# The low halves of streamed weights, made by a negated copy and an adding DMA in place of a subtraction

## The chip, the cores and the metric

The kernel runs on one core of one Trainium2 chip. The time is device microseconds of one execution of the program; fewer is better. The engines of the core are TensorE (PE in the profile), VectorE (DVE), ScalarE (ACT), GpSimd (POOL) and SyncE (SP, which only issues DMAs here). Each has its own queue of instructions and works through it in order; an instruction that waits for a semaphore holds up all that stands behind it on its engine.

## The reference

One layer of a hybrid backbone over 1,024 latent tokens of width 1,024 and 256 context tokens, all in fp32. What matters here is where its matrix products lie:

```python
u = h * (1 + sc1) + sh1                            # modulated tokens
p = u @ w_in + b_in                                # 1024 x 9280: q, k, v, o, gates of mLSTM and GLA
h_m = bidirectional mLSTM (8 heads of 128) of silu(short_conv(q, k)), v, gates
h_g = bidirectional GLA   (4 heads, 128 keys, 256 values) of q, k, v, decay
y_m = (head_norm(h_m) * sigmoid(o)) @ w_branch_mlstm
y_g = (head_norm(h_g) * silu(z)) @ w_branch_gla
mix = (sigmoid(gate_a) * y_m + sigmoid(gate_b) * y_g) @ w_out
h = layer_norm(ALPHA * h + g1 * mix)
gate, val = split((h * (1 + sc2) + sh2) @ w_up + b_up)      # D_FF = 2816
f = (gelu(conv3x3(gate)) * val) @ w_down + b_down
out = layer_norm(ALPHA * h + g2 * f)
```

## The kernel before

Each large product is made of three: both factors are split into a high part (the fp32 value rounded to the type that TensorE multiplies fast, written fp32r) and a low part (what the rounding left), and TensorE adds up high by high, high by low and low by high in one PSUM bank. `mm3` does this over the blocks of 128 rows; its three matmuls are lines 288, 289 and 290 of the profile (1083 to 1085 in the down projection).

Weights are streamed from HBM by `wload`. A call fetches one column block of 256 of a weight matrix in parts of two row blocks. For each part it takes a `raw` tile (four of them in a ring), SyncE loads it (256 KB, line 268), ScalarE copies it into a tile of the ring of `whi` (six tiles, the high part, line 257), and VectorE subtracts: raw minus high, into a tile of the ring of `wlo` (six, the low part, line 258). Each is 128 x 512. Most calls have four parts, because the inner dimension is 1,024; those of the down projection have one. 314 parts go into the two rings; eight parts of `w_out` and the last six parts of `w_down` go into tiles of their own (`s`, `u`, `wlate`), and all 328 pass through `raw`. With six tiles in a ring and four parts in a call, parts 0 and 1 of the next call find a free tile early, and parts 2 and 3 wait until TensorE has read parts of the call before.

The stages follow one another: modulation and log gates (to 230 us), four GLA heads (230 to 545), eight mLSTM heads in pairs (545 to 1115: a value projection for a pair, then query and key for each head, `ml_scan` between), output gates and branches (1115 to 1530), output projection (to 1630), the 22 blocks of the gated unit with its 3x3 convolution on VectorE (1630 to 2110), and the down projection (from 2110), whose last two column blocks are done by token tiles.

The order of instructions on each engine is not the order of the code: the framework's scheduler places them by its own estimate of when each can start, and it also gives out the tiles of a ring in that order. So a change of one instruction's engine moves others.

`split` also serves other places (the gated heads, `kk`, `qq`, `s`; ScalarE and GpSimd, also lines 257 and 258), which are not touched. In the mLSTM, `ml_scan` has GpSimd multiply and add tiles of 128 x 1024 (lines 695, 699, 701), ScalarE take exponentials (698, 702), and VectorE run short chains of Newton steps on 128 x 8 (`mrs`, lines 238 to 243).

Of the kernel before, what the change touches and what calls it, by code (L numbers as in the profile page):

```python
# [6 lines left out]
F32 = mybir.dt.float32  # L7
# [22 lines left out]
EPS = 1e-5  # L30
# [6 lines left out]
def layer_kernel(ctx, tc, I, out, dbg=None):  # L37
# [26 lines left out]
    def slot(i, shape, dt=F32):  # L64
        # 8, 9 and 10, 11 are halves of one tile each, taken in this order
        if i in (8, 9, 10, 11) and sl is sl0:
            n = 1
            for w in shape[1:]:
                n *= w
            tag = "kk" if i < 10 else "qq"  # L70
            if i % 2 == 0:
                half[tag] = sl.tile([P, 2, n], dt, tag=tag, name=nm(tag))
            v = half[tag][0:shape[0], i % 2, :]
            return v if len(shape) == 2 else v.rearrange("p (a b) -> p a b", b=shape[2])
        return sl.tile(shape, dt, tag=f"s{i}", name=nm(f"s{i}"))
# [10 lines left out]

    # ---------------------------------------------------------------- constants
    scn = ExitStack()
# [20 lines left out]

    # masks  # L110
    V.tensor_tensor(xi[:], ti[:], si[:], op=ALU.bitwise_xor)
# [11 lines left out]

    # small vectors, gathered as rows and turned into columns on the tensor engine
    pk0 = [(I["c"][0], 8), (I["c_ctx"], 8), (I["b_mod"][0:2048], 16)]
# [22 lines left out]

    # ---------------------------------------------------------------- modulation for the token mixing
    list(pack(pk0, 0))  # L150
# [20 lines left out]

    # gates, one row of the projection for each: the 32 of the linear attention three times, the 32 of the mLSTM
    raw = slot(7, [P, KD, P])
# [41 lines left out]

    # biases and norm factors in the scaled form in which they are used
    V.tensor_scalar(colB[:, c_om:c_om + 8], colB[:, c_om:c_om + 8], 0.5, None, op0=ALU.mult)
# [8 lines left out]

    # convolution of the bias with the taps, and what the taps beyond the ends would add
    cvb = cst.tile([P, 3, 16], F32, name="cvb")
# [6 lines left out]

    # ---------------------------------------------------------------- helpers
    def newton(y, v, tmp):
# [9 lines left out]
    def rsqrt1(y, h, var, tmp):  # L247
        # of one column, with h = -(var + EPS) / 2
        V.tensor_scalar(h, var, EPS, -0.5, op0=ALU.add, op1=ALU.mult)
        V.tensor_scalar(y.bitcast(I32), h.bitcast(I32), -0.5, float(0x5F3759DF - (1 << 30) - (1 << 22)),  # L250
                        op0=ALU.mult, op1=ALU.add)
        for _ in range(3):
            V.scalar_tensor_tensor(tmp, y, h, y, op0=ALU.mult, op1=ALU.mult)
            V.scalar_tensor_tensor(y, tmp, 1.5, y, op0=ALU.add, op1=ALU.mult)
# [5 lines left out]
    def wload(segs, nk=KD, k0=0, eng=V, into=None):  # L260
        parts = []
        for k4 in range(0, nk, 2):
            n = min(2, nk - k4)
            raw = stg.tile([P, 2, 256], F32, tag="raw", name=nm("raw"), bufs=4)
            r0 = (k0 + k4) * P
            wid = 0
            for src, c0, w, dst in segs:
                SY.dma_start(raw[:, 0:n, dst:dst + w],
                             src[r0:r0 + n * P, c0:c0 + w].rearrange("(k p) c -> p k c", p=P))
                wid = max(wid, dst + w)  # L270
            if into is None:
                hi = stg.tile([P, 2, 256], F32R, tag="whi", name=nm("whi"), bufs=6)
                lo = stg.tile([P, 2, 256], F32R, tag="wlo", name=nm("wlo"), bufs=6)
            else:
                hi, lo = (t[k4 // 4][:, k4 % 4:k4 % 4 + 2, :] for t in into)
            split(hi[:, 0:n, 0:wid], lo[:, 0:n, 0:wid], raw[:, 0:n, 0:wid], eng)
            parts.append((hi, lo))

        def w(k, c, n):
            hi, lo = parts[k // 2]  # L280
            return hi[:, k % 2, c:c + n], lo[:, k % 2, c:c + n]
        return w
# [8 lines left out]

    # ---------------------------------------------------------------- modulated tokens, channel-major, split
    uh = [ubt(k, [P, SEQ], F32R) for k in range(KD)]
# [33 lines left out]

    # ---------------------------------------------------------------- gates
    L = SEQ + CTX
    gr = slot(6, [96, L], F32R)  # L330
    gm = slot(15, [P, L])
    for b in range(3):
        for k in range(KD):
            if b < 2:
                c_ = slice(b * 512, b * 512 + 512)
                make_u(xt[4 * b:4 * b + 4], k, uh[k][:, c_], ul[k][:, c_], 0)
            else:
                make_u(ct, k, cuh[k // 4][:, k % 4, :], cul[k // 4][:, k % 4, :], 1)
        p = proj(lambda k, c, n: tuple(t[:, k % 4, :] for t in gwt[k // 4]), 0, b)
        # high parts, low parts, high parts  # L340
        o = slice(b * 512, b * 512 + BW[b])
        A.activation(gr[0:96, o], p[0:96, 0:BW[b]], AF.Identity, bias=gb[0:96, :])
        V.scalar_tensor_tensor(gr[32:64, o], p[32:64, 0:BW[b]], gb[32:64, :], gr[32:64, o].bitcast(F32),
                               op0=ALU.add, op1=ALU.subtract)
        A.activation(gm[96:128, o], p[96:128, 0:BW[b]], AF.Identity, bias=gb[96:128, :])

    # weights of the log forget gates of the gated linear attention: high, high, low parts
    gws = []
# [12 lines left out]
    def log_gates(h):  # L361
        # by direction, then the context of both
        for parts in (((0, 0), (0, 1)), ((1, 0), (1, 1)), ((0, 2), (1, 2))):
# [22 lines left out]
    def ml_gates():  # L386
        # gates of the mLSTM: rows of the two directions, each in its own storage order
        lf = slot(8, [64, L])
# [66 lines left out]

    # ---------------------------------------------------------------- projections
    def vbias(off):
# [47 lines left out]
    def gla_scan(h, q, k, v):  # L505
# [3 lines left out]
        for d in range(2):  # L509
            SY.dma_start(et[d][:], la_d[d][h][:])  # L510
            A.activation(et[d][:], et[d][:], AF.Exp, scale=1.0 / TAU)
            V.tensor_tensor(qq[:, d, :], et[d][:, 0:SEQ], q[:], op=ALU.mult)
        # context: what is left of the decay after each position
        ze = zero[:].to_broadcast([P, CTX - 1])
# [7 lines left out]
        A.activation(kk[:, 1, 0:SEQ], k[:, 0:SEQ], AF.Copy)  # L522
        # scores inside a chunk: blocks of hs positions against their sibling, from small to large;
        # q carries the decay from its block's border, k the decay to it
        am = slot(12, [P, 8, P])
# [7 lines left out]
        def pairs(t, d0, hs, o, n):  # L533
            # of 2 * hs positions the first half from direction d0, the second from the other one
            a = t[:, d0, o:o + 1]
# [4 lines left out]
        for l in range(7):  # L540
# [13 lines left out]
            for d, eng in ((0, V), (1, G if l % 2 else V)):  # L554
# [7 lines left out]
                eng.tensor_tensor(e4[:, :, 0, 0], e4[:, :, 0, 0], e4[:, :, 1, 0], op=ALU.mult)  # L562
        # whole chunks
        dec2 = sc.tile([P, 2, 8], F32, tag="gdec", name=nm("gdec"), bufs=2)
# [3 lines left out]
        for c0 in (8, 0, 4):  # L568
            for t in (sf, sb):
# [4 lines left out]
                A.activation(t[:, c0 * P:(c0 + n) * P].rearrange("p (c t) -> p c t", t=P), p[:, 0:n, :], AF.Copy)  # L574
        # states
        sbs = [slot(13 + i, [P, 4, 256]) for i in range(2)]
# [20 lines left out]
        def heads(g):  # L597
# [11 lines left out]
            for i in range(4):  # L609
                sq = sc.tile([P, 256], F32, tag="hn", name=nm("sq"), bufs=3)  # L610
                A.activation(sq[:], po[i // 2][:, i % 2, :], AF.Square, accum_out=ss[:, 0, i:i + 1])
            # 1 / sqrt(mean + EPS), with one step of Newton after the tables
            h_, y, m = ss[:, 1, :], ss[:, 2, :], ss[:, 3, :]
# [37 lines left out]
    def ml_proj_qk(h):  # L651
        w = wload([(w_in, O_QM + h * P, P, 0), (w_in, O_KM + h * P, P, P)])
        res = []
        for i in range(2):
# [8 lines left out]
            for b in range(2 + i):  # L663
# [8 lines left out]
                if b == 1:  # L672
                    tap(o, ed[:], t0)
                    tap(o - 1, p[:, 0:1], t2)
                # no neighbour at the ends
                if b != 1:
# [137 lines left out]

    # ---------------------------------------------------------------- output gates, branches, merge
    md_d = drt("md_d", [4096])
# [55 lines left out]
    for j2 in range(4):  # L872
        w = wload([(I["w_branch_gla"], j2 * 256, 256, 0)])
        for e in range(2):
# [11 lines left out]
            mod_row(j, acc)  # L886
    # columns of the gated unit
    rowF = ubt(19, [P, 3, P])
# [40 lines left out]

    # ---------------------------------------------------------------- output projection, first norm  # L930
    lt = ExitStack()
# [82 lines left out]

    # ---------------------------------------------------------------- convolutional gated unit
    ft = ExitStack()
# [42 lines left out]

    # ---------------------------------------------------------------- down projection, second norm  # L1060
    fin = ctx.enter_context(tc.tile_pool(name="fin", bufs=1))
# [11 lines left out]

    # column blocks of one group of rows of w_down after the other, in chunks of two row tiles
    todo = [(g, cb_, k) for g, (k0, k1) in enumerate(((0, N_RES), (N_RES, NF))) for cb_ in range(4)
# [71 lines left out]

    # the last two column blocks, by token tiles
    ahead(len(todo) - len(late))
# [45 lines left out]
```

## Time and profile before

| | |
|---|---|
| median of 3 runs | 2389.48 us (2388.05 to 2392.11) |
| profiled execution, span | 2388.8 us |
| TensorE busy | 2272.9 us, 95% |
| VectorE busy | 1429.5 us, 60% |
| ScalarE busy | 693.9 us, 29% |
| GpSimd busy | 347.7 us, 15% |
| DMA | 231 MB moved, mean 97 GB/s |

The profile is one execution. Rows of its groups read: line, engine, operation, output from input, shape, count, then busy time, mean ns of one, then the engine's idle time just before these instructions and what ended most of it. Rows of the timeline begin with the start in us and the duration. A matmul's row can overlap the next one's, since they are pipelined.

### The profile page before, as it was taken

How to read it: one execution, taken by the hardware profiler on the slowest of the kernel's cores; microseconds unless marked ns; L12 is line 12 of the kernel's file. 1: busy time of each engine (PE TensorE's matmuls, PEld its weight loads, DVE VectorE, ACT ScalarE, POOL GpSimd, SP SyncE). 2: the span in 40 equal slices, each digit the busy share in tenths (PEclk: the TensorE clock that was granted, in tenths of full speed). 3: DMA queues.
4: the chain of work that ended last, by engine and by line, in shares of the span. 5: the costliest groups of instructions: out<-in, count | busy, mean ns of one | idle time of the engine just before them, and what ended most of it. 6: DMA issues, size and time to landing. Idle time of an engine off the chain costs nothing. (4 is left out here: it accounts for less than half of the span.)

```text
span 2388.8 us, 33413 instructions
## 1 busy us (share of the span) xinstructions
PE 2272.9 (95%) x13093; PEld 1970.4 (82%) x13093; DVE 1429.5 (60%) x2664; ACT 693.9 (29%) x1107; POOL 347.7 (15%) x240
## 2 busy tenths in 40 slices
PE   8899999999889888998999999999999999989998
PEld 3788897988788777886886788898888888879998
DVE  4867647274956838656345544576655565567557
ACT  2563233233212223122431233313333333320110
POOL 2101101021220302202110032101011000025300
PEclk9999999999999999999999999999999999999999
DMA  7341021212222212222356644512111222145511
GB/s 254 82 145 49 30 64 43 74 47 60 74 70 75 72 54 83 65 85 91 93 160 215 207 136 154 190 63 71 53 54 39 68 71 78 65 136 177 207 54 63
DMA packets 192351, 231.12 MB, mean 97 GB/s; under 512 B 18577, under 2 KB 149265, under 8 KB 192193
## 3 DMA queue, kind: packets, MB, share of 16 engines
q1 hardware_dynamic: 190321, 222.43, 29.5%
q0 software_dynamic: 1728, 6.29, 0.8%
q8 instruction: 103, 1.69, 0.3%
q14 instruction: 55, 0.45, 0.1%
q10 hardware_dynamic: 144, 0.26, 0.0%
HBM read 183.52 MB, written 45.25 MB: 96 GB/s over the span
## 5 line engine op out<-in xcount | busy, mean ns | idle before, releaser
L288 PE MATMUL pj<-u,whi 128*128 128x512 f32 (+1 forms) x848 | 327.7, 386 | 30.2 <-DVE s L677 21.4
L258 DVE TENSOR_TENSOR wlo<-raw,whi 128x512 fp32r<-128x512 f32 x314 | 230.0, 736 | 204.1 <-ACT whi L257 200.4
L257 ACT ACTIVATE whi<-raw 128x512 fp32r<-128x512 f32 x314 | 197.0, 631 | 481.4 <-PE pj L290 181.5
L289 PE MATMUL pj<-u,whi 128*128 128x512 f32 (+1 forms) x848 | 327.2, 386 | 4.4 <-POOL u L308 3.3
L290 PE MATMUL pj<-u,wlo 128*128 128x512 f32 (+1 forms) x848 | 325.4, 384 | 0.0
L288 PE MATMUL pj<-s,whi 128*128 128x512 f32 x784 | 305.6, 390 | 0.0
L290 PE MATMUL pj<-s,wlo 128*128 128x512 f32 x784 | 305.6, 390 | 0.0
L1047 DVE SCALAR_TENSOR_TENSOR acc<-g,colF,acc 128x945 f32<-128x945 f32 (+2 forms) x168 | 205.0, 1220 | 155.7 <-ACT acc L1038 153.5
L289 PE MATMUL pj<-s,whi 128*128 128x512 f32 x744 | 290.2, 390 | 2.3 <-POOL s L1002 2.3
L288 PE MATMUL pj<-whi,u 128*128 128x256 f32 x768 | 222.5, 290 | 18.1 <-DVE s L647 18.1
L289 PE MATMUL pj<-wlo,u 128*128 128x256 f32 x768 | 221.8, 289 | 2.8 <-DVE wlo L258 2.8
L290 PE MATMUL pj<-whi,u 128*128 128x256 f32 x768 | 221.7, 289 | 0.0
L288 PEld LDWEIGHTS pj<-u,whi 128*128 128x128 f32 x848 | 162.9, 192 | 60.2 <-issue 32.0
L289 PEld LDWEIGHTS pj<-u,whi 128*128 128x128 f32 x848 | 162.9, 192 | 35.5 <-POOL u L308 6.4
L290 PEld LDWEIGHTS pj<-u,wlo 128*128 128x128 f32 x848 | 162.6, 192 | 28.0 <-issue 0.9
L290 PEld LDWEIGHTS pj<-s,wlo 128*128 128x128 f32 x784 | 147.2, 188 | 32.4 <-issue 1.7
L288 PEld LDWEIGHTS pj<-s,whi 128*128 128x128 f32 x784 | 147.2, 188 | 31.9 <-issue 0.9
L289 PEld LDWEIGHTS pj<-s,whi 128*128 128x128 f32 x744 | 139.7, 188 | 33.6 <-POOL s L1002 3.6
L288 PEld LDWEIGHTS pj<-whi,u 128*128 128x128 f32 x768 | 150.6, 196 | 18.6 <-issue 18.6
L289 PEld LDWEIGHTS pj<-wlo,u 128*128 128x128 f32 x768 | 150.7, 196 | 3.0 <-DVE wlo L258 3.0
L290 PEld LDWEIGHTS pj<-whi,u 128*128 128x128 f32 x768 | 150.3, 196 | 0.0
L661 DVE SCALAR_TENSOR_TENSOR s<-pj,colB,s 128x511 f32<-128x511 f32 (+2 forms) x96 | 57.6, 611 | 62.3 <-ACT s L666 61.7
(463 smaller groups left out, 4513.5 us busy)
## 6 DMA issues: line engine op xcount, KB each, us to landing
u<-in_w_mod_dram SPq DMA_DIRECT2D x48, 512.0 KB
raw<-in_w_in_dram SPq DMA_DIRECT2D x96, 256.0 KB
raw<-in_w_up_dram SPq DMA_DIRECT2D x176, 128.0 KB
raw<-in_w_in_dram SPq DMA_DIRECT2D x96, 128.0 KB
raw<-in_w_down_dram SPq DMA_DIRECT2D x44, 256.0 KB
s<-rr SPq DMA_DIRECT2D x16, 512.0 KB
qq<-re SPq DMA_DIRECT2D x16, 512.0 KB
gl<-val SPq DMA_DIRECT2D x12, 512.0 KB
```

The source lines that it names most:

```text
L257: A.activation(hi, src, AF.Copy)
L258: eng.tensor_tensor(lo, src, hi.bitcast(F32), op=ALU.subtract)
L288: T.matmul(p, lh, rh, start=k == 0, stop=False)
L289: T.matmul(p, lh, rl, start=False, stop=False)
L290: T.matmul(p, ll, rh, start=False, stop=k == nk - 1)
L661: V.scalar_tensor_tensor(y[:, o:o + src.shape[1]], src, t, y[:, o:o + src.shape[1]], op0=ALU.mult, op1=ALU.add)
L1047: V.scalar_tensor_tensor(av, g[:, r0 + dy:r1 + dy, c0 + dx:c1 + dx], convw(3 * ky + kx, f), av, op0=ALU.mult, op1=ALU.add)
```

## The change

In `wload` the call of `split` goes. ScalarE makes the high part as before and then a second copy of it with the sign turned, into the low part's tile; then GpSimd issues a DMA from the raw tile to the low part's tile that adds what it carries to what lies there. The low part is now minus high plus raw. The argument that named the subtracting engine is no longer read there. (The comments that the diff also drops are left out.)

```diff
-            split(hi[:, 0:n, 0:wid], lo[:, 0:n, 0:wid], raw[:, 0:n, 0:wid], eng)
+            h_, l_, r_ = hi[:, 0:n, 0:wid], lo[:, 0:n, 0:wid], raw[:, 0:n, 0:wid]
+            A.activation(h_, r_, AF.Copy)
+            A.activation(l_, h_.bitcast(F32), AF.Copy, scale=-1.0)
+            G.dma_start(l_, r_, accum_op=ALU.add)
             parts.append((hi, lo))
```

Every line from there on moves down by three: L702 becomes L705, L865 becomes L868. The new instructions are L277 (high part), L278 (negation) and L279 (DMA). Counted over the program, VectorE loses 328 instructions of 128 x 512, ScalarE gains 328, GpSimd's queue gains 328 DMA issues; on TensorE 683 rows of its order stand elsewhere, on SyncE 108, most of them before 230 us, where the gates' instructions of heads and log decays are interleaved anew.

On ScalarE, before the first mLSTM head (about 543 us; `whi_725` and `whi_728` are parts 2 and 3 of a call, `s6_773` is the tile of which L702 takes the exponential once GpSimd has written it), before:

```order
L257 ACTIVATE whi_725_4710<-raw_724_4707 128x512
L702 ACTIVATE s6_773_5098<-s6_773_5098 128x1024
L257 ACTIVATE whi_728_4717<-raw_727_4714 128x512
L257 ACTIVATE whi_749_4909<-raw_748_4906 128x512
L257 ACTIVATE whi_752_4916<-raw_751_4913 128x512
L666 ACTIVATE s0_730_4721<-pj_731_4722,cvb_289,colB_276 128x512
```

and now:

```order
L277 ACTIVATE whi_725_4756<-raw_724_4753 128x512
L705 ACTIVATE s6_773_5150<-s6_773_5150 128x1024
L278 ACTIVATE wlo_726_4757<-whi_725_4756 128x512
L277 ACTIVATE whi_728_4764<-raw_727_4761 128x512
L277 ACTIVATE whi_749_4957<-raw_748_4954 128x512
L278 ACTIVATE wlo_729_4765<-whi_728_4764 128x512
L278 ACTIVATE wlo_750_4958<-whi_749_4957 128x512
L277 ACTIVATE whi_752_4965<-raw_751_4962 128x512
L278 ACTIVATE wlo_753_4966<-whi_752_4965 128x512
```

The negation into `wlo_726` stands behind the exponential L705, and both DMAs follow their negations on GpSimd.

On GpSimd, where the gated heads are split (about 1390 to 1405 us; `kk_1640` and `qq_1667` hold low parts of heads 0 to 3, `u18` their values, `s0` to `s3` their high parts), before:

```order
L258 TENSOR_TENSOR kk_1640_11147<-u18_1642_11150,s0_1639_11146 128x512 x2
L258 TENSOR_TENSOR kk_1640_11147<-u18_1649_11214,s1_1647_11211 128x512 x2
L258 TENSOR_TENSOR qq_1667_11300<-u18_1669_11303,s2_1666_11299 128x512 x2
L258 TENSOR_TENSOR qq_1667_11300<-u18_1676_11367,s3_1674_11364 128x512 x2
L258 TENSOR_TENSOR s12_1694_11453<-u18_1696_11456,s4_1693_11452 128x512 x2
```

and now:

```order
L258 TENSOR_TENSOR kk_1640_11295<-u18_1642_11298,s0_1639_11294 128x512 x2
L258 TENSOR_TENSOR kk_1640_11295<-u18_1649_11362,s1_1647_11359 128x512 x2
L258 TENSOR_TENSOR qq_1667_11452<-u18_1669_11455,s2_1666_11451 128x512 x2
L279 DMA wlo_1689_11597<-raw_1687_11594 128x512
L279 DMA wlo_1692_11604<-raw_1690_11601 128x512
L279 DMA wlo_1711_11741<-raw_1709_11738 128x512
L279 DMA wlo_1714_11748<-raw_1712_11745 128x512
L258 TENSOR_TENSOR qq_1667_11452<-u18_1676_11519,s3_1674_11516 128x512 x2
```

The adding DMAs of parts 2 and 3 (`wlo_1689`, `wlo_1692`) stand behind the subtractions of the third head's two halves; their negations on ScalarE stand behind the same head's high parts.

On ScalarE, at the end of the down projection (about 2298 to 2312 us; `u10`, `u11` and `wlate` are the resident tiles of the last column block), before:

```order
L257 ACTIVATE u10_2730_19238<-raw_2731_19239 128x512
L257 ACTIVATE whi_2706_19134<-raw_2705_19132 128x512
L257 ACTIVATE u11_2732_19243<-raw_2733_19244 128x512
L257 ACTIVATE wlate_2734_19248<-raw_2735_19249 128x512
L257 ACTIVATE whi_2725_19228<-raw_2724_19226 128x512
L257 ACTIVATE wlate_2736_19253<-raw_2737_19254 128x512
L257 ACTIVATE wlate_2738_19258<-raw_2739_19259 128x512
L257 ACTIVATE wlate_2740_19263<-raw_2741_19264 128x512
L257 ACTIVATE whi_2728_19234<-raw_2727_19232 128x512
```

and now:

```order
L277 ACTIVATE whi_2725_19548<-raw_2724_19546 128x512
L278 ACTIVATE wlo_2726_19549<-whi_2725_19548 128x512
L277 ACTIVATE u11_2732_19566<-raw_2733_19567 128x512
L278 ACTIVATE u11_2732_19566<-u11_2732_19566 128x512
L277 ACTIVATE wlate_2734_19572<-raw_2735_19573 128x512
L278 ACTIVATE wlate_2734_19572<-wlate_2734_19572 128x512
L277 ACTIVATE whi_2728_19555<-raw_2727_19553 128x512
L278 ACTIVATE wlo_2729_19556<-whi_2728_19555 128x512
L277 ACTIVATE wlate_2736_19578<-raw_2737_19579 128x512
L278 ACTIVATE wlate_2736_19578<-wlate_2736_19578 128x512
L277 ACTIVATE wlate_2738_19584<-raw_2739_19585 128x512
L278 ACTIVATE wlate_2738_19584<-wlate_2738_19584 128x512
```

The high part of `raw_2727` has moved ahead of the last three resident tiles. The raw tiles are also handed on otherwise: before, `raw_2733` took the tile of `raw_2731` and `raw_2741` that of `raw_2724`; now (`raw_2731` still takes that of `raw_2702`) `raw_2735` takes that of `raw_2731`, and `raw_2741` that of `raw_2735`. A raw tile is free once its DMA has been carried out, where it was free after the subtraction.

## The prediction

> **What bounds the kernel now.** I read the busy times first, then the stages, what TensorE waits for, and last the single places where a freshly made low part meets the matmul that needs it. The page's head, and its groups for the two instructions of the change:
>
> ```profile
> span 2388.8 us, 33413 instructions
> PE 2272.9 (95%) x13093; PEld 1970.4 (82%) x13093; DVE 1429.5 (60%) x2664; ACT 693.9 (29%) x1107; POOL 347.7 (15%) x240
> L258 DVE TENSOR_TENSOR wlo<-raw,whi 128x512 fp32r<-128x512 f32 x314 | 230.0, 736 | 204.1 <-ACT whi L257 200.4
> L257 ACT ACTIVATE whi<-raw 128x512 fp32r<-128x512 f32 x314 | 197.0, 631 | 481.4 <-PE pj L290 181.5
> ```
>
> TensorE is busy 95% of the span. The table by stretches (first pair: length, PE busy; the fourth is DVE) says where it is not:
>
> ```profile
> 545.00:1115.00 570.00, 512.12 (x3143) 457.57 (x3142) 381.60 (x950) 143.27 (x229) 100.31 (x51) 0.95 0.24 72
> 1630.00:2110.00 480.00, 477.67 (x2121) 394.90 (x2121) 288.85 (x301) 175.81 (x235) 29.44 (x14) 1.00 0.20 62
> ```
>
> In the gated unit (1630 to 2110) 2.3 us of 480 are idle: nothing taken off VectorE can be won there. 57.9 of the idle microseconds lie in the mLSTM. TensorE's list of waits (instruction, what it waited for: us, times, longest) names the largest, and shows that in the whole program it waits only once for a subtracted low part:
>
> ```profile
> PE pj L288 <- DVE s L677: 21.4, 2, 10.9
> PE pj L289 <- DVE wlo L258: 2.8, 1, 2.8
> ```
>
> **What is removed.** 328 subtractions (314 in the row above, 14 into resident tiles) of 0.736 us, 241 us of VectorE. The gain is what of it stood ahead of a wait of TensorE. In the mLSTM little did: before the long stalls VectorE works through tiny norm steps while GpSimd holds the ports with large multiplications:
>
> ```profile
> 633.73 2.27 DVE L240 SCALAR_TENSOR_TENSOR mrs<-mrs 128x8 f32<-128x8 f32 x1
> 638.33 0.17 DVE L239 TENSOR_TENSOR mrs<-mrs 128x8 f32<-128x8 f32 x1
> 633.63 4.64 POOL L699 TENSOR_TENSOR qq<-qq,s 128x1024 f32<-128x1024 f32 x2
> ```
>
> A step of 128x8 takes 2.27 us under L699 and 0.17 after it. Subtractions stand after this chain, not in it (three of them behind 640.47). One order change goes the other way: at head 1 the eight L770 and L682 (before L679) now precede a convolution tap that stood ahead of them. I book 2 us of gain and 2 us of loss, with 0 to 15 of gain as the bound. The 2.8 us above go too, but the DMA that replaces that subtraction is about as late (its negation waits behind an evacuation), so I book none.
>
> **What is added on ScalarE.** 328 negations of 0.631 us, 207 us: 694 becomes 901 of 2389, no bound by itself. Each counts where it lies between a release and a landing. Behind a negation on ScalarE stand evacuations of TensorE's results; 0.6 us is less than the time for which TensorE fills another bank.
>
> **What is added on GpSimd.** 328 DMA issues, and the transfers. No accumulating DMA runs before. The nearest rows are its twelve plain loads of 512 KB from the same queue:
>
> ```profile
> L1066 POOL DMA_DIRECT2D gl<-gl x12: 527/586/743, 2126.9 to 2229.3; - x12
> DMA to landing us min/median/max: 3.7/5.2/9.0
> ```
>
> On GpSimd that is 328 x 0.59 = 192 us of issues, beside 348 of its own work; behind an issue that waits stand its own multiplications (at 543 both L699), pushed by 1 to 3 us, for which I find no matmul due that soon and book nothing. Landing (call it L) comes 3.7 us after the issue when alone, 9.0 when queued behind another. A new DMA reads 256 KB of raw, reads 256 KB of destination and writes 256 KB: 768 KB of traffic against 1,024 for a load, in the same 128 rows, but a sum per element. Its price lies between 3.7 (or a little under, for fewer bytes) and 9.0; I take 4.4, midway between the least and the median row, since in most stages the other DMA traffic is light (share 0.20 in the gated unit).
>
> **Where L is hidden.** Parts 0 and 1 of a load are made 20 us or more ahead. Parts 2 and 3 wait until the previous load's buffers are read, and are tight. In the gated unit:
>
> ```profile
> 1868.12 0.39 PE L290 MATMUL pj<-s,wlo 128*128 128x512 f32 x1
> 1869.06 1.26 ACT L257 ACTIVATE whi<-raw 128x512 fp32r<-128x512 f32 x2
> 1875.60 0.39 PE L290 MATMUL pj<-s,wlo 128*128 128x512 f32 x1
> ```
>
> The buffer is free at 1868.51, its new content is needed at 1875.60: 7.09 us. High part 1869.06 to 1869.7, negation to 1870.3, 0.1 for semaphores, 4.4: lands at 1874.8, 0.8 early. This budget repeats in most of the 69 four-part loads, so the cover is gone from L = 5.2 on. The reload of raw (SyncE) now waits for the landing too; it has over 15 us.
>
> **Where it is not hidden** (price at 4.4):
>
> At 323, after a value projection:
>
> ```profile
> 323.49 0.63 ACT L257 ACTIVATE whi<-raw 128x512 fp32r<-128x512 f32 x1
> 324.98 0.61 ACT L257 ACTIVATE whi<-raw 128x512 fp32r<-128x512 f32 x1
> 327.13 0.28 PE L289 MATMUL pj<-wlo,u 128*128 128x256 f32 x1
> 327.85 0.28 PE L289 MATMUL pj<-wlo,u 128*128 128x256 f32 x1
> ```
>
> 324.98 + 0.61 + 0.74 + 4.4 = 330.7 against 327.85: **2.9 us**. The next head repeats it at 441: **2.9**. The head before has more room:
>
> ```profile
> 227.67 0.64 ACT L257 ACTIVATE whi<-raw 128x512 fp32r<-128x512 f32 x1
> 231.62 0.28 PE L289 MATMUL pj<-wlo,u 128*128 128x256 f32 x1
> ```
>
> 227.67 + 1.35 + 4.4 = 233.4: **1.8**.
>
> At 543 the negation stands behind L702 (now L705) on ScalarE, which waits for GpSimd's L701:
>
> ```profile
> 546.24 1.06 ACT L702 ACTIVATE s<-s 128x1024 f32<-128x1024 f32 x1 [2.53 <-POOL s L701]
> 548.23 0.39 PE L290 MATMUL pj<-u,wlo 128*128 128x512 f32 x1
> ```
>
> 547.3 + 0.7 + 4.4 = 552.4: **4.2**.
>
> At 1398, where the gated heads are split, both new instructions stand behind others: the negation behind the third pair of L257 copies and L862 on ScalarE, the DMA behind the two subtractions that take these copies on GpSimd:
>
> ```profile
> 1397.16 1.37 ACT L257 ACTIVATE s<-u 128x512 fp32r<-128x512 f32 x2 [1.03 <-DVE u L865]
> 1397.87 3.44 POOL L258 TENSOR_TENSOR qq<-u,s 128x512 fp32r<-128x512 f32 x2 [1.47 <-ACT s L257]
> 1398.53 0.48 PE L290 MATMUL po<-u,wlo 128*128 128x512 f32 x1
> ```
>
> GpSimd is through at 1401.3, or 0.8 sooner without VectorE's subtractions beside it: 1400.6 + 4.4 = 1405.0: **6.5**.
>
> At the end the raw ring binds, not the low part's: each of the last loads waits for an earlier tile to be free, then takes 2.9 us (released at 2303.70, used at 2306.61):
>
> ```profile
> 2293.42 0.63 ACT L257 ACTIVATE whi<-raw 128x512 fp32r<-128x512 f32 x1 [5.13 <-PE pt L1085]
> 2303.01 0.69 DVE L258 TENSOR_TENSOR u<-raw,u 128x512 fp32r<-128x512 f32 x1 [2.47 <-ACT u L257]
> 2306.61 0.63 ACT L257 ACTIVATE wlate<-raw 128x512 fp32r<-128x512 f32 x1 [1.03 <-DMA raw<-in_w_down_dram]
> 2318.78 0.28 PE L1083 MATMUL pt<-wlate,u 128*128 128x256 f32 x1
> ```
>
> In the changed program raw_2702, 2731, 2735 and 2741 share one tile. Each link costs 1.35 + 4.4, and 2.9 between links: 2293.42 + 4 x 5.75 + 3 x 2.9 = 2325.1 against 2318.78: **6.3**, with four L in it.
>
> Smaller: 0.6 at each of three mLSTM heads (part 2 from 695.36 to 700.52 and like it), 0.9 at two places in the branches: **2.7**.
>
> Sum: 2.9 + 2.9 + 1.8 + 4.2 + 6.5 + 6.3 + 2.7 = 27.3, and 2388.8 + 27.3 = 2416. The profiled execution lies 0.7 us under the median of the runs, 2389.5, so I say 2416, +1.1%. At L = 3.7 the same sums give 18, at 5.2 about 38.
>
> The Trainium skill, page "DMA: Bandwidth & Descriptors", section "Anatomy of one DMA", counts a DMA from GpSimd as 2.0 us fixed plus its bytes over 436 GB/s: an estimate of 2.6 us for 256 KB. By it the places above would lose 9 us in all, 2398. The rows here, 3.7 at the least for 512 KB against 3.2 by that rule, stand above it, so the sum goes by the rows.
>
> **Rivals.** (a) Late everywhere: from L = 5.2 the parts of every four-part load are late. For it: the median row is 5.2, and adding may be slower than copying; against it: those rows move a third more and often run in pairs. At 6.2 the places above cost 52 and the others about 30: 2471; at 9.0 another 2.8 us in each of 69 loads: about 2665. (b) VectorE was a bound: in the mLSTM it loses 63 subtractions, 42.9 us (first pair of this row, of that line alone):
>
> ```profile
> 545.00:1115.00 570.00, 42.86 (x63) 0.95 0.24 72
> ```
>
> If two thirds of it, 28 us, came out of the stalls (21.4 us before L677 alone), that is, with L at 3.7, 2389 + 18 - 28 = 2379. It decides once the stalls give back more than the 18; against it stands that these chains hold no subtraction. (c) The same at half to two thirds of that size: gain and loss cancel, about 2389. (d) VectorE's port: GpSimd and VectorE delay each other in the rows above, and a stall of the issue by one such step, 2.3 us, makes L 6.7 and all loads late: about 2510.
>
> The rule behind (d) is also that of the Trainium skill, page "SBUF — State Buffer", section "Who interferes with whom": some forms of VectorE shut GpSimd out for a whole instruction, and the writing of descriptors then waits. The issues of the row above, 527 to 743 ns beside a busy VectorE, do not show it.
>
> **How the numbers follow.** Forecast (L between 3 and 5.2, small gains) 0.66, of 2395 to 2428; (a) 0.14 and (d) 0.04, above 2428; (b) 0.08; (c) 0.08. A measurement of this kernel tells 0.2%, 4.8 us, from no change. The range for 8 in 10 reaches from 2392 to 2480: below it lie (b), (c), above it an L over 6.2. Faster is (b), same (c), slower the rest.
>
> **What would show it.** Right: a landing of 4 to 5 us for the new DMA; no wait of TensorE for it in the gated unit; waits of 2 to 7 us near 230, 327, 445, 548, 1398 and 2318; ScalarE near 900 and VectorE near 1190 busy. Wrong: a landing over 5.2 with a wait of TensorE in every load; mLSTM stalls that shrink by more than 5 us in all, or new stalls before 230, where the order of the gates' instructions changes most and I booked nothing.

## The result, and the profile after

The changed kernel takes 2465.39 us, the median of four executions (2463.07 to 2468.17), against 2388.77 for the kernel before, measured on the same chip: a ratio of 1.0326, 95% interval 1.0309 to 1.0343. That is 77 us more, inside the range given; the forecast was 27. The profiled execution took 2463.07 us, 1.8 above its span.

The head of the page of the changed kernel (span; then busy time, share and instructions of each engine), and its row for the mean granted clock of TensorE:

```profile
span 2461.3 us, 34236 instructions
PE 2298.6 (93%) x13093; PEld 1984.9 (81%) x13093; DVE 1228.6 (50%) x2336; ACT 868.3 (35%) x1435; POOL 626.8 (25%) x568
core 0: 2461.3 us, clock 0.972
```

VectorE lost 201 us and ScalarE gained 174, GpSimd 279. The span grew by 72.5: TensorE is idle for 162.7 us where it was idle for 115.9 (+47), and is busy 25.7 us longer with the same 13093 matmuls, because its granted clock fell from 0.983 to 0.972: in the records of the clock, 0.50 was granted for 82 us in all before and for 140 after.

The groups of the two new instructions (busy, mean ns, idle before), the issue of the ring's adding DMAs in the view of its line (ns min/median/max), their landing times, and the same by stage (the last column is the median; the branches with the output projection, then the gated unit):

```profile
L278 ACT ACTIVATE wlo<-whi 128x512 fp32r<-128x512 f32 x314 | 195.3, 627 | 6.0
L279 POOL DMA_DIRECT2D wlo<-raw x314 | 273.4, 905 | 998.9 <-ACT wlo L278 759.6
L279 POOL DMA_DIRECT2D wlo<-raw x314: 852/862/1633, 64.6 to 2379.7; - x157
DMA to landing us min/median/max: 3.2/4.5/10.7
wlo<-raw POOLq DMA_DIRECT2D x54, 256.0 KB, 5.0
wlo<-raw POOLq DMA_DIRECT2D x96, 256.0 KB, 3.9
```

The landing is what was assumed, 4.5 against 4.4; an issue takes 0.86 us and not 0.59. The last two rows show that the landing differs by stage. The DMA queues of the changed kernel show the load that the adding DMAs bring (packets, MB, share of the sixteen engines; SyncE's queue is `q1`, GpSimd's `q0`):

```profile
q1 hardware_dynamic: 190321, 222.43, 27.8%
q0 software_dynamic: 48960, 92.30, 22.2%
```

Before, the GpSimd queue held twelve loads and 0.8%. Less those, 328 adding DMAs have 47,232 packets, 144 each, and 22.2% x 2461.3 x 16 - 0.8% x 2388.8 x 16 = 8,437 engine-microseconds: 179 ns a packet, 25.7 us a DMA, 527 us of all sixteen engines.

The list of what TensorE waits for after (total, times, longest), and beside it two rows that the prediction did not show of the list before (numbers of lines are three lower there):

```profile
PE pj L291 <- DVE s L680: 28.8, 3, 9.7
PE pt L842 <- DVE u L837: 15.2, 5, 4.1
PE pj L293 <- DMA wlo<-raw: 11.8, 6, 4.1
PE pa L555 <- ACT s L549: 10.4, 3, 5.0
PE pj L292 <- DMA wlo<-raw: 6.4, 7, 2.3
PE pj L292 <- DMA s<-raw: 4.8, 1, 4.8
PE po L1087 <- DMA wlo<-raw: 3.8, 1, 3.8
PE po L293 <- DMA wlo<-raw: 2.5, 1, 2.5
...
PE pt L839 <- DVE u L834: 6.4, 4, 2.0
PE pa L552 <- ACT s L546: 2.5, 3, 1.4
```

The five rows with a DMA come to 29.3 us in 16 waits: adding DMAs that land late. Two more rows have grown, by 8.8 and 7.9, and no adding DMA is in them: L842 waits for the modulation rows (the adaLN products of streamed `w_mod`), L555 for attention scores that ScalarE makes after a store.

Where the loss arises, from the start of the same matmul (by its place in TensorE's order) in both traces:

| stage (us before) | lost there | by the prediction |
|---|---|---|
| modulation and log gates (to 210) | 2.6 | 0 |
| GLA (to 611, the first mLSTM projection in it) | 18.0 | 11.8 |
| mLSTM (to 1163) | 4.9 | 1.8 |
| output gates (to 1254) | 0.0 | 0 |
| branches (to 1520) | 27.4 | 7.4 |
| output projection (to 1548) | 11.0 | 0 |
| gated unit and most of the down projection (to 2297) | 1.9 | 0 |
| the end | 6.4 | 6.3 |
| sum | 72.1 | 27.3 |

In the branches the table by stretches (length; busy time of PE, PEld, DVE, ACT, POOL with counts; granted clock; DMA share; GB/s) reads so, first two stretches of before, then two of after, which hold about the same matmuls:

```profile
1275.00:1300.00 25.00, 23.08 (x94) 17.10 (x95) 12.37 (x19) 4.85 (x8) 1.05 (x2) 1.00 0.77 247
1325.00:1355.00 30.00, 26.67 (x111) 19.70 (x110) 15.52 (x23) 4.74 (x8) 0.53 (x1) 1.00 0.71 229
```

```profile
1300.00:1330.00 30.00, 25.87 (x94) 18.12 (x95) 11.74 (x17) 7.47 (x12) 3.21 (x5) 0.89 0.89 263
1360.00:1400.00 40.00, 32.74 (x118) 23.13 (x117) 15.00 (x21) 7.58 (x13) 4.83 (x6) 0.85 0.83 234
```

The engines were already busy to 0.71 and 0.77 there, with `w_mod`, gates and heads beside the weights; now to 0.83 and 0.89. 94 matmuls in 25 us became 94 in 30, and 111 in 30 us became 118 in 40.

One stall of this stage from near (the matmul that ended it on TensorE, then the table for some of the microseconds around it):

```profile
1302.32 0.58 PE L293 MATMUL pj<-s,wlo 128*128 128x512 f32 x1 [4.14 <-DMA wlo<-raw]
1300.00:1302.00 2.00, 0.00 (x0) 0.00 (x0) 0.38 (x1) 0.00 (x0) 0.00 (x0) 1.00 1.07 336
1304.00:1306.00 2.00, 1.32 (x2) 0.12 (x2) 0.58 (x1) 0.63 (x1) 0.00 (x0) 0.50 1.13 214
1306.00:1308.00 2.00, 2.00 (x5) 1.24 (x5) 0.68 (x1) 0.00 (x0) 0.00 (x0) 0.50 1.05 335
1310.00:1312.00 2.00, 2.00 (x10) 1.65 (x9) 0.49 (x1) 0.00 (x0) 0.53 (x1) 1.00 0.60 224
```

The shares of 1.05 to 1.13 leave no engine time free (where a share is over 1, times of packets overlap, so it is no exact load). TensorE waits 4.14 us; then the clock is granted at 0.50, and the next full 2 us hold five matmuls and not ten. From before the stall to some ten microseconds after it, the same matmuls came to lie 7.6 us later against the trace of before (a second gap of 0.93 us, at 1304.7, is in it). The Trainium skill, page "TensorE: Matmul & The Clock Gate", section "Part 1: The HAM clock gate", gives the array half its clock after an idle window of about 3.4 us, until it has been busy for as long; this stall agrees (0.50 after 4.14 us of idleness, 1.00 again at 1310). Shorter waits of this trace do not go by that length alone. One of 2.63 us at 567 brought the half clock too:

```profile
567.22 0.50 PE L293 MATMUL pj<-u,wlo 128*128 128x512 f32 x1 [2.63 <-DMA wlo<-raw]
570.00:572.00 2.00, 2.00 (x6) 1.56 (x5) 0.18 (x1) 0.78 (x1) 0.00 (x0) 0.50 1.13 175
```

After waits of 2.91 us at 1434 and of 2.53 at 1451 the clock stayed at 1.00.

### The profile page after: what moved, and what is told of

It is laid out like the page before. It is cut to its first block, busy times and chain, and to the rows that moved or that the text cites. A ratio compares the mean times of both kernels' runs of the same rounds, so it can differ in the third digit from the quotient of the medians.

```text
span 2461.3 us, 34236 instructions
## 1 busy us (share of the span) xinstructions
PE 2298.6 (93%) x13093; PEld 1984.9 (81%) x13093; DVE 1228.6 (50%) x2336; ACT 868.3 (35%) x1435; POOL 626.8 (25%) x568
## 3 DMA queue, kind: packets, MB, share of 16 engines
q0 software_dynamic: 48960, 92.30, 22.2%
## 4 chain that ended last, share of the span: by engine, by line
PE 66%; DVE 12%; DMA 10%; issue 9%; ACT 1%; POOL 1%; SPq 0%; DVEq 0%; POOLq 0%; ACTq 0%
PE pj L293 14%; PE pj L292 13%; PE pj L291 13%; DMA wlo<-raw 3%; PE pa L555 2%; PE pt L732 1%; PE po L752 1%; DMA u<-in_w_mod_dram 1%; PE pa L291 1%; PE po L753 1%; PE pa L292 1%; PE pa L293 1%; PE pt L596 1%; PE po L293 1%; PE po L291 1%
## 5 line engine op out<-in xcount | busy, mean ns | idle before, releaser
L279 POOL DMA_DIRECT2D wlo<-raw x314 | 273.4, 905 | 998.9 <-ACT wlo L278 759.6
L291 PE MATMUL pj<-u,whi 128*128 128x512 f32 (+1 forms) x848 | 329.5, 389 | 29.9 <-DVE s L680 28.8
L277 ACT ACTIVATE whi<-raw 128x512 fp32r<-128x512 f32 x314 | 192.8, 623 | 390.6 <-PE pj L293 170.3
L291 PE MATMUL pj<-whi,u 128*128 128x256 f32 x768 | 221.3, 289 | 17.9 <-DVE s L650 16.3
L278 ACT ACTIVATE wlo<-whi 128x512 fp32r<-128x512 f32 x314 | 195.3, 627 | 6.0
L291 PEld LDWEIGHTS pj<-whi,u 128*128 128x128 f32 x768 | 150.4, 196 | 18.7 <-issue 16.9
```

Of the source, the lines that this page charges most:

```text
L277: A.activation(h_, r_, AF.Copy)
L278: A.activation(l_, h_.bitcast(F32), AF.Copy, scale=-1.0)
L279: G.dma_start(l_, r_, accum_op=ALU.add)
L291: T.matmul(p, lh, rh, start=k == 0, stop=False)
```

## The experiments

Theory A says that the adding DMAs' load on the sixteen engines delays other transfers and themselves. Its rivals: the wait for the landing as such, ScalarE's negations (later a longer hold of the `raw` tiles, called H, and GpSimd's queue, called Q). "Lost" below is against the kernel before in the same comparison.

### side_hold: the load beside the old subtraction

The kernel before, with one adding DMA more for each part, which reads the high part and adds it into `raw` when the subtraction is done. No matmul needs it.

```diff
         split(h_, l_, r_, V)
+            G.dma_start(raw[:, 0:n, 0:wid], hi[:, 0:n, 0:wid].bitcast(F32), accum_op=ALU.add)
```

> The subtraction stays on VectorE as before; behind it GpSimd issues an adding DMA of the same size per part (high part added into the raw tile, which is then dead), so that traffic, GpSimd issues and the longer hold of the raw tile are all there, but no matmul waits for the landing and ScalarE has no negation. Theory A (side effects of the transfers in the stages that already stream much: branches near 1300 to 1440 and output projection near 1590 cost about 33 of the 77 us): about 2420, with the lost time in those two stages. Rival B (the loss is the wait of TensorE for the landing itself and what the clock loses after it): within 6 us of 2389.

2476.12 us, ratio 1.0361 [1.0342, 1.038]: 86 lost, more than by the change, though the subtraction stands where it stood and no matmul waits for the new DMA. From its list of TensorE's waits:

```profile
PE pt L840 <- DVE u L835: 19.2, 6, 4.8
PE pa L553 <- ACT s L547: 12.3, 3, 4.7
```

These are the two waits that had grown in the changed kernel. Rival B falls; A's own figure, about 2420, was too low by 56. What the DMA does to others is enough for a loss of this size; its own lateness is not needed. The place is not the same throughout: by the table's stages 32.0 us are lost in the branches (the change: 27.4), but 22.8 between 1548 and 2297, where the change lost 1.9, and nothing of that in the gated unit.

### side_tiny: the same DMA over four elements of a row

```diff
+            G.dma_start(raw[:, 0, 0:4], hi[:, 0, 0:4].bitcast(F32), accum_op=ALU.add)
```

> As side_hold, but each adding DMA carries only four elements per partition (128 rows of 16 bytes instead of 2 KB): the raw tile is held until a landing as before and GpSimd issues as often, but little is moved. If the side effects are the hold of the raw tile and of SyncE's queue behind it: as slow as side_hold, about 2420. If they are the load on the DMA engines: within 6 us of 2389.

2414.43, ratio 1.010 [1.0079, 1.012]: 24 lost. Theory A had at most 6 here, so it is not the whole: issues, completions, the hold of `raw` and a light load cost 24 us together. The GpSimd queue and the landing (min/median/max):

```profile
q0 software_dynamic: 48960, 6.98, 3.8%
DMA to landing us min/median/max: 2.0/2.7/7.8
```

The same packets with 16 bytes each take 3.8% of the engines. From this kernel to side_hold, which differs only in bytes, are 62 us.

### neg_dveadd: the negation alone

```diff
-            G.dma_start(l_, r_, accum_op=ALU.add)
+            V.tensor_tensor(l_, l_.bitcast(F32), r_, op=ALU.add)
```

> ScalarE negates as in the changed kernel, but VectorE adds the raw tile to it (no DMA). Theory: the 328 negations delay ScalarE's copies L549 in two of the linear-attention heads (5.0 and 3.6 us of waiting there in the changed kernel against 1.5 us before): about 2397, with those waits and nothing in the branches. Rival: the negations are free everywhere and those waits came from the DMAs: within 4 us of 2389.

2394.87, ratio 1.0021 [1.0008, 1.0033]: 5 lost, between the two expectations, with all the negations on ScalarE. The waits for L549 come to 5.3 us here, against 2.5 before and 10.4 in the changed kernel.

### neg_dve: the adding DMA alone, negated on VectorE

```diff
-            A.activation(l_, h_.bitcast(F32), AF.Copy, scale=-1.0)
+            V.tensor_scalar(l_, h_.bitcast(F32), -1.0, None, op0=ALU.mult)
```

> The adding DMA as in the changed kernel, but VectorE makes the negation instead of ScalarE. Theory (negations on ScalarE cost the two waits for L549, about 8 us): about 2457. Rival (those waits come from the DMAs or from the new order): 2465 and the waits stay.

2504.57, ratio 1.0469 [1.044, 1.0497]: 114 lost, 37 more than with ScalarE; neither expectation had this. The wait at L555 stays without any negation on ScalarE:

```profile
PE pa L555 <- ACT s L549: 12.4, 3, 4.3
```

So the adding DMA makes that wait without any negation on ScalarE, and ScalarE's negations alone make at most a small part of the loss. Why VectorE's are so much worse than its subtractions was not pursued.

### side_free: the load without the hold of raw

As side_hold, but the DMA adds into a tile that nothing uses; to make room for it two other rings are shorter.

```diff
+    scr = stg.tile([P, 2, 256], F32, name="scr")
+    G.memset(scr[:], 0.0)
...
+            G.dma_start(scr[:, 0:n, 0:wid], hi[:, 0:n, 0:wid].bitcast(F32), accum_op=ALU.add)
...
-            u = lp.tile([P, 512], F32, tag="u", name=nm("u"), bufs=3)
+            u = lp.tile([P, 512], F32, tag="u", name=nm("u"), bufs=2)
...
-            z = fin.tile([P, 256], F32, tag="z", name=nm("z"), bufs=4)
+            z = fin.tile([P, 256], F32, tag="z", name=nm("z"), bufs=2)
```

> As side_hold (subtraction on VectorE, an adding DMA of 256 KB per part beside it), but the DMA adds the high part into a scratch tile, so the raw tile is free after the subtraction as before. The load on the DMA engines is that of side_hold. (Two other rings are a tile or two shorter to make room, and the DMAs wait for one another because they share the scratch tile.) Theory H (the raw tile's hold makes SyncE's reload wait, and what stands behind it in SyncE's queue is late): at most 25 us over before, 2390 to 2415. Theory A (load on the DMA engines): 50 us or more over, 2440 to 2475.

2468.15 against 2388.51, ratio 1.0337 [1.0322, 1.0353]: 80 lost. The reload of `raw` no longer waits for the DMA, and the loss stays, so H falls. What the shorter rings cost by themselves was not measured; they act behind the output projection, and ahead of it the stages agree with side_hold's (210 to 611: 13.3 lost against 11.7; branches: 30.0 against 32.0).

### raw5: five raw tiles

```diff
-            raw = stg.tile([P, 2, 256], F32, tag="raw", name=nm("raw"), bufs=4)
+            raw = stg.tile([P, 2, 256], F32, tag="raw", name=nm("raw"), bufs=5)
```

The rings `u` and `z` are shortened as in side_free.

> The changed kernel with five raw tiles instead of four (the same two other rings shorter). Theory H: reloads wait less for the landing, so the losses in linear-attention heads, branches, output projection and tail shrink: about 2425 to 2440. Theory A: 2460 to 2470, since the traffic is the same.

2466.98, ratio 1.0329 [1.0314, 1.0345]: as the changed kernel. H falls a second time.

### hg_act: another queue for the stores of the GLA heads

```diff
-                SY.dma_start(hg_d[2 * h + e][:, g * 512:g * 512 + 512], hr[:, e, :])
+                A.dma_start(hg_d[2 * h + e][:, g * 512:g * 512 + 512], hr[:, e, :])
```

> The changed kernel, but the stores of the linear-attention outputs (hg, line 633) are issued by ScalarE, which also writes their source, instead of SyncE. In the changed kernel these stores stand behind raw reloads on SyncE, and the copies L549 wait for them. Theory H: the two waits for L549 near 374 and 497 fall from 5.0 and 3.6 us to about 1.5, and the time to about 2457. Theory A or ScalarE's load: they stay and the time stays at 2465 or rises.

2469.1, ratio 1.0346 [1.0328, 1.0363]: nothing won. The waits for L549 are 3.06, 3.21 and 3.90, where the changed kernel has 1.76, 5.04 and 3.61: 10.2 in all against 10.4. A wait of 4.13 for a low part is new, at 441.8 in this trace. The queue that issues the store is not what makes it late.

### ffn_only: the change in the gated unit alone

```diff
+            if segs[0][0] is I["w_up"]:
                 A.activation(h_, r_, AF.Copy)
                 A.activation(l_, h_.bitcast(F32), AF.Copy, scale=-1.0)
                 G.dma_start(l_, r_, accum_op=ALU.add)
+            else:
+                split(h_, l_, r_, V)
```

> Negation and adding DMA only in the 22 loads of the gated unit (88 of 328 parts), the subtraction on VectorE everywhere else. By the trace of the changed kernel nothing is lost there: 2389, within 4 us either way. If the landings hurt there in a way that only the whole sum shows: above 2395.

2390.12, ratio 1.0009 [1.0, 1.0019]: nothing lost or won that is clear of the noise, where the DMA share was 0.20 before and is 0.48 in the changed kernel.

### side_plain: the same bytes, copied and not added

```diff
+            G.dma_start(raw[:, 0:n, 0:wid], hi[:, 0:n, 0:wid].bitcast(F32))
```

> As side_hold, but the DMA beside the subtraction copies the high part over the dead raw tile instead of adding it: the same bytes carried, the same issues, the same hold. A packet of the adding DMA took 179 ns of an engine in the changed kernel; a plain packet of 2 KB took 84 ns before. Theory A1 (the engines' time counts): about half of side_hold's 86 us, 2425 to 2440. Theory A2 (the bytes or the number of DMAs count): 2465 to 2475, as side_hold.

2422.49 against 2387.63, ratio 1.0152 [1.0133, 1.0171]: 35 lost, just under the band expected of engine time, and far from the 86 of the adding DMA with the same bytes. Its GpSimd queue, its issues and its landing:

```profile
q0 software_dynamic: 27968, 92.30, 10.6%
L277 POOL DMA_DIRECT2D raw<-whi x314: 538/538/1038, 65.5 to 2341.9; - x157
DMA to landing us min/median/max: 2.2/2.8/7.4
```

The same 92.30 MB in 80 packets a DMA take 11.6 engine-microseconds each, an adding DMA 25.7; the issue takes 0.54 and not 0.86, the landing 2.8 and not 4.5. So most of the price is in the adding, not in the number of bytes.

### early_only: only parts that have time

Adding DMAs for parts 0 and 1 of four-part loads; parts 2 and 3 subtracted on VectorE.

```diff
+            if nk == 8 and k4 < 4:
                 A.activation(h_, r_, AF.Copy)
                 A.activation(l_, h_.bitcast(F32), AF.Copy, scale=-1.0)
                 G.dma_start(l_, r_, accum_op=ALU.add)
+            else:
+                split(h_, l_, r_, V)
```

> Adding DMAs only for parts 0 and 1 of the four-part loads, which have 20 us of room; VectorE subtracts for parts 2 and 3 and in the down projection. So half the DMAs and no late landing. Theory A (load on the DMA engines): 2410 to 2430. Rival B (landings on the path, with what the clock loses after each): within 6 us of 2389.

2409.81, ratio 1.0093 [1.0077, 1.0108]: 22 lost, at the lower edge of what A gave. Two of its waits, the counterparts of L555 and L842 in the changed kernel (three lines further down here), 2.5 and 6.4 us before:

```profile
PE pa L558 <- ACT s L552: 9.3, 3, 3.5
PE pt L845 <- DVE u L840: 7.8, 5, 2.1
```

Parts with 20 us of room cost time too, and TensorE waits for no adding DMA here but once, for 0.2 us. A loss does not need a late landing.

### calm: no adding in the stage with the full engines

`adding[0]` is set to False ahead of the branches and back to True behind the output projection; in between VectorE subtracts.

```diff
+            if adding[0]:
                 A.activation(h_, r_, AF.Copy)
                 A.activation(l_, h_.bitcast(F32), AF.Copy, scale=-1.0)
                 G.dma_start(l_, r_, accum_op=ALU.add)
+            else:
+                split(h_, l_, r_, V)
```

> The changed kernel, but in the branches and the output projection (from the mLSTM's end to the gated unit) the subtraction stays on VectorE. If the loss belongs to the stage in which it shows: 2465 less about 38, 2427. If it only moves to other stages or comes from the order as a whole: above 2440.

2425.67, ratio 1.0154 [1.0135, 1.0174]; 2427 was expected. The loss of these two stages, 38 us by the table above, is gone (nothing is lost there in its trace), and the other 38 us are there. The branches in its table by stretches:

```profile
1300.00:1330.00 30.00, 29.03 (x122) 22.17 (x121) 15.76 (x23) 5.58 (x9) 1.05 (x2) 1.00 0.73 237
```

122 matmuls in 30 us at a DMA share of 0.73, against 94 at 0.89. The loss belongs to the stage in which the DMAs run, not to something earlier.

### tiny_add: the change with the traffic taken out

```diff
-            G.dma_start(l_, r_, accum_op=ALU.add)
+            G.dma_start(l_[:, 0, 0:4], r_[:, 0, 0:4], accum_op=ALU.add)
```

> The changed kernel with its negations, issues, waits and order, but each adding DMA carries only four elements per partition (the low part of the rest stays minus the high part, so the output is not the reference's). Landing about 2.7 us instead of 4.5, and almost no traffic. Theory A: 2395 to 2415, the other 50 to 70 us being the traffic. Rival (issues, holds and negations cost it): above 2435.

2403.4, ratio 1.0061 [1.0042, 1.008]: 16 lost. Negations, issues, waits for a landing, and order are all as in the change, with a landing of 2.6 us. So 61 of the 77 are the bytes that are added: their engine time, and the later landing that goes with it. What stays lies in GLA (4.2), the branches (5.2) and the output projection (5.8, with a wait of 4.1 for `s<-raw`). The wait at L555 is back at its old size:

```profile
PE pa L555 <- ACT s L549: 1.1, 3, 0.7
PE pj L293 <- DMA wlo<-raw: 3.8, 3, 1.8
```

### thin_after and thin_before: fewer bytes of w_mod

Both kernels with the streamed modulation weights cut to 128 of 512 columns (shown for the changed one).

```diff
-            SY.dma_start(raw[:], I["w_mod"][k2 * P:(k2 + 2) * P, c0:c0 + 512].rearrange("(k p) c -> p k c", p=P))
+            SY.dma_start(raw[:, :, 0:128], I["w_mod"][k2 * P:(k2 + 2) * P, c0:c0 + 128].rearrange("(k p) c -> p k c", p=P))
...
-                V.scalar_tensor_tensor(acc[:], raw[:, i, :], sC[:, k2 + i, 0:1], acc[:], op0=ALU.mult, op1=ALU.add)
+                a4 = acc[:].rearrange("p (a c) -> p a c", c=128)
+                V.scalar_tensor_tensor(a4, raw[:, i, 0:128].unsqueeze(1).to_broadcast([P, 4, 128]), sC[:, k2 + i, 0:1], a4,
+                                       op0=ALU.mult, op1=ALU.add)
```

> The changed kernel, but the stream of w_mod in the branches is cut to a quarter of its columns (128 of 512, used four times, so the modulation rows are not the reference's); VectorE does as many products as before. Theory A says that the 27 us lost between 1163 and 1427 us of the kernel before come from the adding DMAs and this stream competing for the DMA engines: then most of it goes, and the time is 2465 less 15 to 25, about 2445. If the place of the loss is the adding DMAs' own landing and order: at most 6 us less, 2459 or more.

> The kernel before with the same cut of w_mod, for comparison. TensorE waited 6.4 us there for the modulation rows: 2380 to 2386 by theory A; 2389 if that stream never mattered.

2448.83, ratio 1.0247 [1.0228, 1.0266], and 2384.29, ratio 0.998 [0.9969, 0.9991]. With the thin stream the change costs 64.5 us and not 77; in the branches 18 and not 27. So competition with `w_mod` is some 9 to 12 us of the loss, and two thirds of the branches' share is something else.

### memset_dve and memset_thin: GpSimd's queue

GpSimd also clears the accumulators of the modulation rows, behind adding DMAs (theory Q). Here VectorE does it; memset_thin has the thin `w_mod` as well.

```diff
-        G.memset(acc[:], 0.0)
+        V.memset(acc[:], 0.0)
```

> The changed kernel, but VectorE clears the accumulator of the modulation rows (line 830) instead of GpSimd. On GpSimd that clearing stands behind the issues of adding DMAs, and the load of b_mod and VectorE's sums wait for it (33 us of waiting in the changed kernel against 8 before). Theory Q (GpSimd's queue is the rest of the branches' loss): 2465 less 8 to 18, about 2452. Theory A alone (competition of transfers): 2462 to 2468, though that wait of VectorE goes.

> Both: VectorE clears, and the stream of w_mod is cut to a quarter. If the two together make the branches' loss: 2384 + 77 less 27, about 2434. If the rest is competition with the other streams of that stage (gates, heads, raw weights): 2445 to 2450, as with the cut alone.

2467.48, ratio 1.033 [1.0303, 1.0357], and 2448.56, ratio 1.0254 [1.0233, 1.0274]: each as without the edit. Q falls, as far as these clearings are its means. Which other streams of the branches (gates `gt` from `thb`, heads, the raw weights, or the adding DMAs one behind another) carry the remaining 18 us was not separated.

No version with the full computation was faster than the kernel before; the nearest, ffn_only, is the same as it.

## Why the prediction was right or wrong

**Right: direction, landing, and where nothing is lost.** The landing was 4.5 by the median against 4.4. That size is in part luck: the rows behind it are plain loads of twice the bytes, and a plain copy of 256 KB lands in 2.8 (side_plain), so 1.7 us are the adding, for which the prediction had no row. (Nor is 9.0 the price of standing behind one other: the first of that pair took 7.9.) In the gated unit TensorE waits for it twice, for 0.9 and 0.6 us, where none was said, and ffn_only lost nothing; there it lands in 3.9, inside the budget of 5.2. ScalarE is busy 868 (900 was said), VectorE 1229 (1190). VectorE's relief won nothing: the mLSTM's waits of TensorE came to 45.1 us (28.8 + 16.3) and not 47.9 (21.4 + 18.1 + 8.4), and the stage as a whole became 4.9 longer. Rival (b) falls with that, (c) too. Rival (d) needed an issue that is held up by VectorE; issues took 852 to 1633 ns, always more than the 527 to 743 of before, but side_plain's 538 says that it is the adding that makes them long. Rival (a) gave 2471, close to the time measured, for a cause that is not there: it has L at 6.2 and late parts in all loads.

**At the places that were named:** each of the six large ones lost time. At 229 it was 1.7 (1.8 said). At 543 and at the end it was 4.8 and 6.4 (4.2 and 6.3), but by two errors that cancel: TensorE waited only 2.6 and 4.4 us there, and the rest is the half clock behind the wait, which the sum did not have. At 323 and 441 it was 1.4 and 1.3, half of the 2.9 each; why was not followed further. At 1398 it was 3.1, half of the 6.5: GpSimd was through with the pair of subtractions at 1447.7, which is 1398.0 against TensorE's matmuls of before and not 1400.6. The wait just ahead of it has another cause:

```profile
1433.67 1.02 PE L842 MATMUL pt<-u,ones 128*1 128x512 f32 x2 [2.91 <-DVE u L837]
1451.06 0.50 PE L293 MATMUL po<-u,wlo 128*128 128x512 f32 x1 [2.53 <-DMA wlo<-raw]
```

Together the six places lost 18.7 us where 24.6 were booked; over 50 of the 72 lie elsewhere. (The sum also set a span, 2388.8, beside times of runs; after, the run's time lies 1.8 us above its span.)

**Wrong: the step that took the DMAs' cost to be their own landing.** The part on GpSimd counts 192 us of issues and a landing; the load on the sixteen engines is named there only to choose L ("in most stages the other DMA traffic is light"). Nothing was booked for transfers that the new ones push back. A row on the page of before could have warned: its GpSimd queue

```profile
q0 software_dynamic: 1728, 6.29, 0.8%
```

has 144 packets for each of twelve DMAs, and 0.8% x 2388.8 x 16 / 1728 = 177 ns a packet, so 25.5 engine-microseconds a DMA; 328 / 16 x 25.5 = 523 us of all engines, 22% of the span. The measured share is that, but by luck: those packets carry 3.6 KB each (6.29 MB / 1728) of a plain load, the new ones 1.8 KB that are added, and side_plain's copies, with 80 packets and 11.6 engine-microseconds each, show that without the adding the load would be less than half. Put into the stage of 1240 to 1600 (62 adding DMAs, 99 us of 360), this makes 0.80 of a share of 0.53 (measured in the same stretch: 0.74), and more where it had been 0.71 already. Four terms failed: the first and the third by this traffic, the second by it in half, the fourth at every wait:

- The branches: 7.4 booked, 27.4 lost. Beside 1398 (3.1) come the landing at 1302 (7.6) and waits of 4.11, 3.62, 3.64 and 2.91 us for L842. That the traffic does it is shown by calm (gone with it) and side_hold (there without the new dependence).
- The output projection: 0 booked, 11.0 lost; one wait of 4.8 us for `s<-raw` and one of 2.3. The traffic is only half of it: tiny_add keeps 5.8 us, and a wait of 4.1 for `s<-raw`.
- GLA: two waits for L549 not booked, 4.3 and 3.9 lost. L549 on ScalarE needs a tile that a store of the head's output still reads. Both traces from L632, which makes that tile, to L549, before and after:

```profile
356.70 1.26 ACT L629 ACTIVATE s<-pt,colB 128x512 f32<-128x512 f32 x2 [1.50 <-PE pt L626]
362.36 1.22 ACT L546 ACTIVATE s<-kk 128x512 f32<-128x512 f32 x2 [3.36 <-DMA hg<-s]
```

```profile
363.74 1.25 ACT L632 ACTIVATE s<-pt,colB 128x512 f32<-128x512 f32 x2
372.96 1.21 ACT L549 ACTIVATE s<-kk 128x512 f32<-128x512 f32 x2 [6.94 <-DMA hg<-s]
```

  4.4 us from the end of the one to the other became 8.0. tiny_add brings the wait back to 1.1 in all, neg_dve leaves it: it is the traffic in the main.
- The price of a stall: the sum counted each gap as its own length. With the clock at 0.50 behind it, the 4.14 us and what followed cost 7.6. The 58 us more at 0.50 are about 29 us of work (an estimate from the two totals, 82 and 140), near the 25.7 by which TensorE's busy time grew, a third of the whole loss.

Of the 77 us, 61 are the added bytes (tiny_add), about 5 the negations (neg_dveadd, if the parts may be added up), and the remaining 11 issues, the wait for a landing of 2.6 us, and order. Shown is that the added bytes do it and in which stages; that other transfers wait for the engines and not for something else on their way is read from shares of 0.8 to 1.1, and was not tried by moving them to engines of their own.

## What to carry to other kernels

Price a new DMA twice: by its landing, and by its packets times the time of one, as a share of the sixteen engines in each stage; then look in the stage with the highest share for what feeds TensorE with little room. The time of a packet of another kind, from the queue's row on the page, tells no more than whether the load is light or heavy: here packets of a plain copy and of an adding one differed, and the row of before hit by luck. Price a wait with the slow clock behind it as well. An engine with half its time free (VectorE here, outside the chain) is not a reason to move its work onto a resource that everyone shares.

## What the runs showed of the hardware

An adding DMA of 256 KB within SBUF takes 2.2 times the engine time of a plain one (25.7 against 11.6 us over the engines, 144 packets against 80), lands in 4.5 us against 2.8, and its issue holds GpSimd for 0.86 us against 0.54. The Trainium skill, page "DMA: Bandwidth & Descriptors", section "Anatomy of one DMA", gives an estimate of 2.6 us for this size; the plain copy comes near it (2.8), the adding one does not. Adding four elements a row still takes 144 packets, and lands in 2.7 us. The loss does not rise evenly with the load: with engine shares of 3.8%, 10.6% and 21.9% for the GpSimd queue, side_tiny, side_plain and side_hold lost 24, 35 and 86 us, 11 for the first 6.8 points more and 51 for the next 11.3. (side_plain also has fewer packets and a shorter issue.)
